# The running sum of exponentials on GpSimd, added in two halves instead of one

## The chip, the cores and the metric

The kernel runs on one core of a Trainium2 chip. The metric is the device time of one execution in microseconds (us); smaller is better. The engines are named as the profile names them: PE is TensorE (matmuls), PEld its weight loads, DVE is VectorE, ACT is ScalarE, POOL is GpSimd, SP is SyncE, which issues most of the DMAs.

## What is computed

One layer of an encoder is applied to two batches of 2048 tokens with the same weights: RMSNorm, one wide input projection, grouped-query attention (8 query heads, 2 key/value heads of 64) beside a Fourier branch, gates, an output projection, an embedding that is gated and added, and a final RMSNorm. The change lies in the softmax of the attention:

```python
def one_block(qblk):
    s = jnp.einsum('bkgqd,bskd->bkgqs', qblk, k).astype(jnp.float32) * scale
    pr = jax.nn.softmax(s, axis=-1).astype(v.dtype)
    return jnp.einsum('bkgqs,bskd->bqkgd', pr, v)
```

The kernel takes the softmax apart: it subtracts a maximum per query inside the matmul, makes the exponentials, multiplies them with the values without dividing, sums them beside that, and divides the product by the sum at the end.

## The kernel before

A first stage, up to about 760 us, loads and scales the weights, normalises the tokens and makes the projections. The second, from 760 to 2500 us, is the attention; the rest of the Fourier branch and the output projection are woven into it. A short tail finishes the last tokens.

The attention works through 64 **units**: a batch, a key/value head and a block of 128 tokens, that is 4 heads x 128 = 512 query columns. A unit has 8 **steps**, and each step takes 256 keys as two times 128. In `scores` a step makes two score tiles of 128x512 in PSUM by PE (line 1317, `ps_s`); ACT turns each into exponentials (line 1320), the first into `p[:, 0]`, the second into `p[:, 1]` of one float32 buffer of 128x2x512. There are seven such buffers (`P32`, tile `p32`), so step g takes the buffer of step g - 7.

POOL keeps the running sum. In step 0 it has nothing to do; in step 1 it adds the buffers of steps 0 and 1 into a fresh `acc` (line 1323), in steps 2 to 7 the new buffer to `acc` (line 1325), each time 128x1024 elements in one instruction. Behind step 7 three short instructions follow: line 1328 adds the two halves of `acc` to each other, 1329 and 1330 split the result into two float16 parts, `acc_h`. Four steps later, in step 4 of the next unit, PE sums `acc_h` over the partitions (`sums`, line 1399), and DVE takes the reciprocal and multiplies (`divide`, lines 1406 and 1407). The exponentials themselves go to PE in groups of four steps (`pv`, line 1383).

DVE takes the row maxima of a later unit (14 steps ahead) from PSUM (`maxima`, line 1355, tile `a_mx`): PE fills one buffer `ps_m` of two banks (line 1347), DVE reduces it, and only then can PE fill it again. Between these, DVE has work of the output projection. Three of its operations are 1024 columns wide and read two operands from SBUF: line 1554 (`mh`, the low part of the mixed branches), line 1703 (`h_hl`, the low part of the hidden state) and line 1689 (`h`, the final norm). `square` and `norm` with `rsqrt` (lines 269 to 284) make the factors of the norms in small operations of 128x2, on DVE for the first token block and at the very end, on POOL otherwise. POOL also multiplies a Fourier tile by its gate (line 1190, `fo`, 128x512, up to about 907 us) and the attention output by its gate (line 1535, `ag`, 128x512), and issues the stores of finished tokens (line 1691).

Each engine works through its instructions in the order in which they stand, and waits for semaphores of the others. In this stage the order on PE, ACT, DVE and SP is that in which the program writes it; that on POOL is made by the scheduler of the language.

Of the kernel before, what the change touches and what calls it, by code (L numbers as in the profile page):

```python
# [14 lines left out]
ALU = mybir.AluOpType  # L15
# [150 lines left out]
class Build:  # L166
# [1102 lines left out]
    def attention(self, kvp):  # L1269
# [3 lines left out]
        nc, st = self.nc, self.st  # L1273
# [3 lines left out]
        kt, vt, Q, P, O, MX, ACC, AT, M4, S, MR, AR = ({} for _ in range(12))  # L1277
# [28 lines left out]
        def scores(u, j):  # L1306
            s, kv, t = units[u]
            P[u, j] = p = pool.tile([128, 2, 512], F32, name="p32", bufs=P32)
            k = kt[s, kv, j // 4]
            todo = [] if j else [(kone, MR.pop(u))]  # L1310
            todo += [(k[:, j % 4, y], Q[u][b]) for y, b in ((1, 0), (1, 1), (2, 0))]
            if j == 0:
                S[u] = [self.psS.tile([128, 512], F32, name="ps_s") for e in range(2)]
            for i, (w, q) in enumerate(todo):
                for e in range(2):
                    sl = slice(64 * e, 64 * e + 64)
                    nc.tensor.matmul(S[u][e][:], w[sl], q[sl].rearrange("p h q -> p (h q)"), start=j == i == 0,  # L1317
                                     stop=i + 1 == len(todo), skip_group_check=True)
            for e in range(2):
                nc.scalar.activation(p[:, e, :], S[u][e][:], AF.Exp, scale=self.sc["s_scale"][:])  # L1320
            if j == 1:
                ACC[u] = pool.tile([128, 2, 512], F32, name="acc", bufs=2)
                nc.gpsimd.tensor_tensor(out=ACC[u][:], in0=P[u, 0][:], in1=p[:], op=ALU.add)  # L1323
            elif j > 1:
                nc.gpsimd.tensor_tensor(out=ACC[u][:], in0=ACC[u][:], in1=p[:], op=ALU.add)  # L1325
            if j == 7:
                acc, AR[u] = ACC.pop(u), pool.tile([128, 2, 512], F16, name="acc_h", bufs=1)
                nc.gpsimd.tensor_tensor(out=acc[:, 0, :], in0=acc[:, 0, :], in1=acc[:, 1, :], op=ALU.add)
                nc.gpsimd.tensor_copy(AR[u][:, 0, :], acc[:, 0, :])
                nc.gpsimd.tensor_tensor(out=AR[u][:, 1, :], in0=acc[:, 0, :], in1=AR[u][:, 0, :], op=ALU.subtract)  # L1330
                del Q[u], S[u]
                if u == last[s, kv]:
                    for b in range(2):
                        del kt[s, kv, b]
# [117 lines left out]
        for g in range(8 * n + 7):  # L1452
            self.step = g
            self.flush()
            u, j = g // 8, g % 8
            if j == 0 and 0 < u and u + 2 < n:
                load_q(u + 2)
            if g == 6:
                load_v(0, 1)
            if j == 4 and u - 1 in fresh:  # L1460
                load_kv(1, fresh[u - 1])
            if 0 <= u < n:
                scores(u, j)
            self.drain(lead(g))
            if j == 4:
                if u + 1 < n:
                    max_rows(u + 1)
                if u > 0:
                    ps = self.bank() if u < n else self.psM.tile([128, 1024], F32, name="ps_m")
                    sums(u - 1, ps[:, 0:256])  # L1470
                    divide(u - 1, ps[:, 0:256])
            heavy = (g - 1) % PVG == PVG - 1 and 0 <= g - 1 < 8 * n
            if heavy:
                self.run_slow(1 if j else 2)
                pv((g - 1) // 8, (g - 1) % 8 - PVG + 1)
            yield 0 if heavy else RATE if g >= 8 * n // 2 else 1 if g > FIRST else SLOW
# [567 lines left out]
```

## Time and profile before

| what | value |
|---|---|
| three runs | 2596.09, 2598.25, 2606.04 us (median 2598.25) |
| the profiled execution | 2597.87 us |
| its span, first to last instruction | 2595.8 us |
| mean granted clock of PE | 0.991 |
| POOL additions of line 1325 | 384, together 927.6 us |
| POOL additions of line 1323 | 64, together 150.8 us |
| exponentials of line 1320 on ACT | 1024, 684 ns each in the mean |
| maxima of line 1355 from `ps_m` on DVE | 498, 1223 ns each in the mean |

A row of a group or of the timeline names the line of the program, the engine, the operation, and what is written from what with its shape. A number in brackets at the end of a row of the timeline is the time for which the engine had been idle, with what ended it. Two instructions of POOL can overlap a little in the record, so what POOL takes for a series is read from the distance of the starts.

### The profile page before, as it was taken

Reading aid. Unit: us, or ns where it says so; the run is one execution under the profiler, and the core shown is the slowest. Engines: PE = TensorE matmul, PEld = TensorE weight load, DVE = VectorE, ACT = ScalarE, POOL = GpSimd, SP = SyncE. Lnnn points to the kernel's source line nnn. Section 1 sums busy time; section 2 is a strip of 40 time slices with the busy share of each in tenths; the row PEclk is TensorE's granted clock in tenths of the full one; section 3 lists DMA queues with packets and bytes.
Section 4 is the critical chain, followed back from the end, with each engine's and each line's share of the span. In section 5 each row is a group of like instructions: output and inputs, shape, how many; then the busy total and the mean of one; then the engine's idle time right before and its main releaser. Section 6 shows DMA issues by size and latency. Waiting matters only on the chain. (4 is left out here: it accounts for less than half of the span.)

```text
span 2595.8 us, 49879 instructions
## 1 busy us (share of the span) xinstructions
PE 2511.0 (97%) x19896; PEld 1384.0 (53%) x19896; DVE 1668.4 (64%) x2382; ACT 1183.6 (46%) x1983; POOL 1896.6 (73%) x1646
## 2 busy tenths in 40 slices
PE   6999989999999999999999999999999999999988
PEld 3566656666656545545545555445544554545533
DVE  7766576777566856566666666666666665766534
ACT  4433353434235545554544545444544444445522
POOL 0465545475659978888888888878887988888840
PEclk9999999999999999999999999999999999999999
DMA  8467588787377742223222233422223322233232
GB/s 259 101 175 198 162 223 230 185 195 180 103 197 248 212 118 62 58 76 78 59 69 75 71 81 88 90 69 63 73 73 82 72 75 63 66 82 76 78 76 53
DMA packets 450265, 297.92 MB, mean 115 GB/s; under 512 B 294000, under 2 KB 394480, under 8 KB 450032
## 3 DMA queue, kind: packets, MB, share of 16 engines
q1 hardware_dynamic: 437952, 256.28, 38.9%
q0 software_dynamic: 12080, 38.46, 4.2%
q8 instruction: 155, 2.54, 0.4%
q14 instruction: 78, 0.64, 0.1%
HBM read 146.12 MB, written 82.45 MB: 88 GB/s over the span
## 5 line engine op out<-in xcount | busy, mean ns | idle before, releaser
L1325 POOL TENSOR_TENSOR acc<-acc,p 128x1024 f32<-128x1024 f32 x384 | 927.6, 2416 | 109.5 <-ACT p L1320 84.6
L1320 ACT ACTIVATE p<-ps_s,s_scale 128x512 f32<-128x512 f32 x1024 | 648.1, 684 | 636.4 <-PE ps_s L1317 613.9
L1355 DVE TENSOR_REDUCE a_mx<-ps_m 128x1 f32<-128x1024 f32 x498 | 608.9, 1223 | 512.0 <-PE ps_m L1347 501.0
L1649 PE MATMUL ps_g<-w_pg,hT 64*128 64x512 f16 x2784 | 494.1, 376 | 3.8 <-DVE seen L1610 2.4
L1383 PE MATMUL ps_o<-p,v 128*64 128x256 f32 x4096 | 468.2, 381 | 0.0
L1317 PE MATMUL ps_s<-q,k 64*128 64x512 f16 x3072 | 433.1, 378 | 1.4 <-ACT p L1320 1.0
L1383 PEld LDWEIGHTS ps_o<-p,v 128*64 128x64 f32 x4096 | 283.7, 137 | 160.4 <-issue 28.5
L504 PEld LDWEIGHTS <-uc 128*128 128x128 f16 x2400 | 236.3, 99 | 231.2 <-DMA uc<-hl 19.5
L1649 PEld LDWEIGHTS <-hT 64*128 64x128 f16 x2784 | 204.8, 94 | 156.9 <-issue 15.7
L1649 PE MATMUL ps_g<-w_wo,mh 64*128 64x512 f16 x1440 | 260.5, 376 | 3.2 <-DVE mh L1554 1.9
L1649 PE MATMUL ps_g<-w_wo,mT 64*128 64x512 f16 x1440 | 257.3, 376 | 0.0
L1317 PEld LDWEIGHTS <-k 64*128 64x128 f16 x3072 | 152.6, 94 | 195.3 <-issue 77.0
L1347 PE MATMUL ps_m<-k,q 64*128 64x512 f16 x996 | 200.8, 377 | 10.2 <-DVE a_mx L1355 9.8
L504 PEld LDWEIGHTS <-w_ga 128*128 128x128 f16 x1536 | 148.8, 98 | 33.5 <-issue 11.9
L1323 POOL TENSOR_TENSOR acc<-p,p 128x1024 f32<-128x1024 f32 x64 | 150.8, 2357 | 11.7 <-ACT p L1320 10.7
L1649 PEld LDWEIGHTS <-mh 64*128 64x128 f16 x1440 | 101.5, 94 | 91.5 <-issue 16.6
L1649 PEld LDWEIGHTS <-mT 64*128 64x128 f16 x1440 | 107.0, 94 | 76.3 <-issue 4.8
L772 POOL TENSOR_TENSOR t<-t,t 128x640 f32<-128x640 f32 x32 | 49.2, 1556 | 121.2 <-DVE t L767 121.2
L1406 DVE RECIPROCAL ps_f<-ps_f 128x256 f32<-128x256 f32 x61 | 107.1, 1756 | 13.6 <-PE ps_f L1399 13.6
L504 PE MATMUL ps_x<-uc,w_ga 128*128 128x256 f16 x1008 | 113.5, 273 | 2.0 <-DVE a_mx L1355 1.4
L504 PE MATMUL ps_x<-w_gf,uc 128*128 128x512 f16 x480 | 108.0, 384 | 2.4 <-DVE a_mx L1355 2.4
L1390 ACT ACTIVATE at<-ps_o,a_scale 128x256 f32<-128x256 f32 x64 | 30.4, 474 | 168.2 <-PE ps_o L1383 168.2
(347 smaller groups left out, 3415.6 us busy)
## 6 DMA issues: line engine op xcount, KB each, us to landing
q<-qTd SPq DMA_DIRECT2D x256, 64.0 KB, 2.2
ag<-agd SPq DMA_DIRECT2D x64, 256.0 KB, 3.5
out<-h POOLq DMA_DIRECT2D x31, 512.0 KB, 3.1
x<-in_x_prompt SPq DMA_DIRECT2D x16, 512.0 KB, 4.9
gfd<-gt POOLq DMA_DIRECT2D x32, 256.0 KB, 2.7
agd<-gat POOLq DMA_DIRECT2D x64, 128.0 KB, 2.8
w_st<-in_w_out SPq DMA_DIRECT2D x32, 256.0 KB, 4.0
w_st<-in_w_ple_gate SPq DMA_DIRECT2D x32, 256.0 KB, 4.0
```

Source lines behind the costliest of these rows:

```text
L504: self.nc.tensor.matmul(ps, lhs(ia, k), rhs(ib, k), start=(i == 0), stop=(i == 3 * ks - 1))
L772: nc.gpsimd.tensor_tensor(out=t1[:, tt], in0=t1[:, tt], in1=t2[:, tt], op=ALU.add)
L1317: nc.tensor.matmul(S[u][e][:], w[sl], q[sl].rearrange("p h q -> p (h q)"), start=j == i == 0, stop=i + 1 == len(todo), skip_group_check=True)
L1320: nc.scalar.activation(p[:, e, :], S[u][e][:], AF.Exp, scale=self.sc["s_scale"][:])
L1323: nc.gpsimd.tensor_tensor(out=ACC[u][:], in0=P[u, 0][:], in1=p[:], op=ALU.add)
L1325: nc.gpsimd.tensor_tensor(out=ACC[u][:], in0=ACC[u][:], in1=p[:], op=ALU.add)
L1347: nc.tensor.matmul(ps[c], Q[u][0][sl, h, :], kt[s, kv, half][sl, :, 0, :], start=True, stop=True)
L1355: nc.vector.reduce_max(MX[u][:, h, half, c:c + 1], x, axis=AX.X)
L1383: nc.tensor.matmul(o[64 * f:64 * f + 64], vt[s, kv, c // 8][:, c % 8, :], p[:, e, f], start=(c == 0), stop=(c == 15))
L1390: nc.scalar.activation(at[:].rearrange("p c q -> p (c q)"), o, AF.Copy, scale=self.sc["a_scale"][:])
L1406: nc.vector.reciprocal(r, r)
L1649: nc.tensor.matmul(g[0][:], g[1](ia, k)[sl], g[2](ib, k)[sl], start=a, stop=z, skip_group_check=True)
```

## The change

Each addition of 128x1024 becomes two of 128x512: one adds `p[:, 0]`, one adds `p[:, 1]`, each to its half of `acc`. The arithmetic is the same. Lines behind it move by one (1328 becomes 1329, 1355 becomes 1356, and so on).

```diff
             if j == 1:
                 ACC[u] = pool.tile([128, 2, 512], F32, name="acc", bufs=2)
-                nc.gpsimd.tensor_tensor(out=ACC[u][:], in0=P[u, 0][:], in1=p[:], op=ALU.add)
-            elif j > 1:
-                nc.gpsimd.tensor_tensor(out=ACC[u][:], in0=ACC[u][:], in1=p[:], op=ALU.add)
+            if j:
+                a, b = ACC[u], P[u, 0] if j == 1 else ACC[u]
+                for e in range(2):
+                    nc.gpsimd.tensor_tensor(out=a[:, e], in0=b[:, e], in1=p[:, e], op=ALU.add)
             if j == 7:
                 acc, AR[u] = ACC.pop(u), pool.tile([128, 2, 512], F16, name="acc_h", bufs=1)
```

POOL before, the end of one unit and the beginning of the next, with the semaphores that an instruction waits for (Activation is ACT's, Pool its own; the number behind `p` is that of a buffer):

```order
L1325 TENSOR_TENSOR acc<-acc,p_10762 128x1024 [waits Activation_49,Pool_49]
L1535 TENSOR_TENSOR ag<-ag 128x512 [waits DMAHW2_49,DMAHW1_49,DVE_49]
L1325 TENSOR_TENSOR acc<-acc,p_10796 128x1024 [waits Activation_49,Pool_49]
L1325 TENSOR_TENSOR acc<-acc,p_10854 128x1024 [waits Activation_49,Pool_49]
L1328 TENSOR_TENSOR acc<-acc 128x512 [waits Pool_49]
L1329 CAST acc_h<-acc 128x512 [waits PE_49,Pool_49]
L1330 TENSOR_TENSOR acc_h<-acc,acc_h 128x512 [waits Pool_49]
L1323 TENSOR_TENSOR acc<-p_10903,p_10938 128x1024 [waits Activation_49]
```

The same place of POOL with the change:

```order
L1326 TENSOR_TENSOR acc<-acc,p_10808 128x512 [waits Activation_49,Pool_49] x2
L1536 TENSOR_TENSOR ag<-ag 128x512 [waits DMAHW2_49,DMAHW1_49,DVE_49]
L1326 TENSOR_TENSOR acc<-acc,p_10843 128x512 [waits Activation_49,Pool_49] x2
L1326 TENSOR_TENSOR acc<-acc,p_10902 128x512 [waits Activation_49,Pool_49] x2
L1329 TENSOR_TENSOR acc<-acc 128x512 [waits Pool_49]
L1330 CAST acc_h<-acc 128x512 [waits PE_49,Pool_49]
L1331 TENSOR_TENSOR acc_h<-acc,acc_h 128x512 [waits Pool_49]
L1326 TENSOR_TENSOR acc<-p_10952,p_10987 128x512 [waits Activation_49] x2
```

Each addition has become two that stand next to each other, and nothing else has moved. A half waits on ACT for its own exponential, and on POOL for its own half of the step before, which is the second instruction back.

At three places of the first units a product of the Fourier branch came to stand between two halves. POOL before, at one of them:

```order
L1325 TENSOR_TENSOR acc<-acc,p_10252 128x1024 [waits Activation_49,Pool_49]
L1190 TENSOR_TENSOR fo<-fo,gf_in 128x512 [waits DMAHW6_49,DVE_49]
L1325 TENSOR_TENSOR acc<-acc,p_10274 128x1024 [waits Activation_49,Pool_49]
L1190 TENSOR_TENSOR fo<-fo,gf_in 128x512 [waits DMAHW7_49,DMAHW3_49,DVE_49]
L1328 TENSOR_TENSOR acc<-acc 128x512 [waits Pool_49]
```

POOL there with the change:

```order
L1326 TENSOR_TENSOR acc<-acc,p_10285 128x512 [waits Activation_49,Pool_49] x2
L1326 TENSOR_TENSOR acc<-acc,p_10308 128x512 [waits Activation_49,Pool_49]
L1190 TENSOR_TENSOR fo<-fo,gf_in 128x512 [waits DMAHW6_49,DVE_49]
L1190 TENSOR_TENSOR fo<-fo,gf_in 128x512 [waits DMAHW7_49,DMAHW3_49,DVE_49]
L1326 TENSOR_TENSOR acc<-acc,p_10308 128x512 [waits Activation_49,Pool_49]
L1329 TENSOR_TENSOR acc<-acc 128x512 [waits Pool_49]
```

The first product has moved behind one half, the second ahead of one. Beside three products of line 1190 one of line 1535 has moved by one half. On PE, ACT, DVE and SP every instruction stands where it stood, with the same waits; only line and buffer numbers differ.

## The prediction

> **What bounds the kernel now.** I read the page's first part, then the busy time by stretches, then who waited for whom on PE.
>
> ```profile
> span 2595.8 us, 49879 instructions
> PE 2511.0 (97%) x19896; PEld 1384.0 (53%) x19896; DVE 1668.4 (64%) x2382; ACT 1183.6 (46%) x1983; POOL 1896.6 (73%) x1646
> ...
> 1000.00:1500.00 500.00, 495.10 (x4350) 255.32 (x4348) 322.07 (x303) 249.84 (x413) 435.59 (x349) 1.00 0.27 68
> 1500.00:2000.00 500.00, 496.60 (x4358) 246.73 (x4356) 314.10 (x286) 247.87 (x406) 421.86 (x368) 1.00 0.32 78
> 2000.00:2500.00 500.00, 498.37 (x4376) 252.23 (x4372) 308.51 (x272) 243.69 (x400) 427.48 (x358) 1.00 0.29 71
> ```
>
> The columns of the last three rows are busy time of PE, PEld, DVE, ACT and POOL, then the granted clock and DMA. The attention stage runs from 760 to 2500 us and holds every instruction that changes. PE is busy 1490.1 of these 1500 us, POOL 1284.9 (86%): POOL is second, and neither DVE (63%) nor ACT (49%) is near. So the change can bring only what PE still waits, and cost only what makes PE wait anew.
>
> ```profile
> PE ps_m L1347 <- DVE a_mx L1355: 6.3, 10, 1.6
> PE ps_s L1317 <- ACT p L1320: 5.0, 4, 4.0
> PE ps_g L1649 <- DVE mh L1554: 1.9, 3, 0.8
> PE ps_g L1649 <- DVE h L1570: 0.5, 2, 0.3
> ...
> PE ps_m L1347 <- DVE a_mx L1355: 3.4, 7, 0.9
> ```
>
> These are PE's waits (us in total, times, longest), first from 930 to 2500 us, and as the last row the largest of 760 to 930. After 930 PE waits 13.7 us in all, and no row names POOL.
>
> **Part one: what the halves cost on POOL.** 448 additions of 1024 columns become 896 of 512.
>
> ```profile
> L1325 POOL TENSOR_TENSOR acc<-acc,p x384: 2340/2353/3439, 771.7 to 2492.0; 128x1024 f32<-128x1024 f32 x192
> L1323 POOL TENSOR_TENSOR acc<-p,p x64: 2336/2357/2379, 766.1 to 2475.0; 128x1024 f32<-128x1024 f32 x64
> L1190 POOL TENSOR_TENSOR fo<-fo,gf_in x32: 1262/1272/1282, 774.0 to 907.1; 128x512 f32<-128x512 f32 x32
> ...
> 774.01 2.50 POOL L1190 TENSOR_TENSOR fo<-fo,gf_in 128x512 f32<-128x512 f32 x2
> 776.47 2.37 POOL L1325 TENSOR_TENSOR acc<-acc,p 128x1024 f32<-128x1024 f32 x1
> ...
> 781.24 7.22 POOL L1325 TENSOR_TENSOR acc<-acc,p 128x1024 f32<-128x1024 f32 x3
> ...
> 793.33 1.26 POOL L1328 TENSOR_TENSOR acc<-acc 128x512 f32<-128x512 f32 x1
> 794.66 0.61 POOL L1329 CAST acc_h<-acc 128x512 f16<-128x512 f32 x1
> ```
>
> By durations the halves look dear: 2 x 1.272 = 2.54 us against 2.353. What counts on a full queue is the spacing. Three additions in a row take 7.22 us, 3 x 2.353 plus two gaps of 0.08: each reads what the one directly ahead wrote. L1328 and L1329, also dependent, leave a gap of 0.07. The two products of L1190 are independent and take 2.50 together, so the second starts 0.04 ahead of the first one's end; from the first of the pair to the next instruction it is 776.47 - 774.01 = 2.46 us. In the changed order a half depends on its own half of the step before, two instructions back. I therefore price a pair at 2.46 against 2.353 + 0.08 = 2.43: +0.03 us a step, 448 x 0.03 = 13 us of POOL time, 0.2 us a unit of seven additions. If every half had the dependent gap, a pair would be 2 x (1.272 + 0.07) = 2.68: +0.25 a step, 1.8 us a unit. Below nothing: with an empty queue the first half starts behind the first of two exponentials, and the last half ends earlier than a whole addition would. I take +0.03, by the nearest row, of the same shape, type and spacing.
>
> The Trainium skill, GPSIMD Engine Reference, section 3.1 "Elementwise — side-by-side cycle accounting", speaks against halving: each instruction pays a dispatch through two software hops, and an element of a two-input operation about 2.6 cycles at 1.2 GHz. By that, 512 columns are 1.11 us, an estimate; the trace's 1.272 leaves 0.16 for the fixed part, and 448 more of them would be some 72 us of POOL time, 1.1 us a unit. The spacing of the L1190 pair says that most of it is hidden behind the instruction ahead.
>
> A unit takes (2475.0 - 766.1) / 63 = 27.1 us, and POOL is idle in 14% of it, 3.9 us. Either price fits. Nor does lateness reach PE:
>
> ```profile
> 2012.94 1.16 POOL L1330 TENSOR_TENSOR acc_h<-acc,acc_h 128x512 f16<-128x512 f32 x1
> ...
> 2014.69 2.38 POOL L1323 TENSOR_TENSOR acc<-p,p 128x1024 f32<-128x1024 f32 x1
> ...
> 2014.71 0.41 PE L1399 MATMUL ps_f<-acc_h,ones 128*64 128x256 f16 x4
> ...
> 2025.18 1.27 ACT L1320 ACTIVATE p<-ps_s,s_scale 128x512 f32<-128x512 f32 x2 [1.04 <-PE ps_s L1317]
> ```
>
> POOL's result goes to PE's sums (L1399), four steps into the next unit, and frees the buffers of the exponentials. This is the tightest place of the 64 units: L1330 ends at 2014.10, PE reads at 2014.71, 0.6 us later. Seven steps on from the buffer that L1323 read, ACT writes it again, 8.1 us after L1323 left it at 2017.07. +0.2 us fits; at +1.8 the tightest units would cost PE about a us each, 5 us for a handful.
>
> **Part two: what the halves free on DVE.**
>
> ```profile
> L1703 DVE SCALAR_TENSOR_TENSOR h_hl<-h,h_r,h_hl 128x1024 f16<-128x1024 f32 x29 | 65.3, 2251 | 1.3 <-ACT h_hl L1699 1.3
> L1554 DVE SCALAR_TENSOR_TENSOR mh<-ag,mix_s,mh 128x1024 f16<-128x1024 f32 x30 | 62.4, 2079 | 0.0
> L1689 DVE SCALAR_TENSOR_TENSOR h<-h,rsh_z,gfin 128x1024 f32<-128x1024 f32 x27 | 61.6, 2280 | 0.0
> ...
> 958.49 1.28 DVE L1703 SCALAR_TENSOR_TENSOR h_hl<-h,h_r,h_hl 128x1024 f16<-128x1024 f32 x1 [1.28 <-ACT h_hl L1699]
> ...
> 1221.20 4.80 POOL L1325 TENSOR_TENSOR acc<-acc,p 128x1024 f32<-128x1024 f32 x2
> 1223.85 3.23 DVE L1703 SCALAR_TENSOR_TENSOR h_hl<-h,h_r,h_hl 128x1024 f16<-128x1024 f32 x1
> 1226.08 2.13 POOL L1328 TENSOR_TENSOR acc<-acc 128x512 f32<-128x512 f32 x1
> 1227.01 2.28 DVE L1689 SCALAR_TENSOR_TENSOR h<-h,rsh_z,gfin 128x1024 f32<-128x1024 f32 x1
> 1229.22 1.21 DVE L1355 TENSOR_REDUCE a_mx<-ps_m 128x1 f32<-128x1024 f32 x1
> 1230.48 0.39 PE L1347 MATMUL ps_m<-k,q 64*128 64x512 f16 x2 [1.56 <-DVE a_mx L1355]
> ...
> 1518.97 0.39 PE L1347 MATMUL ps_m<-k,q 64*128 64x512 f16 x2 [1.56 <-DVE a_mx L1355]
> ```
>
> With POOL idle, L1703 takes 1.28 us; its mean after 930 is 2.25. At 1223.85 it starts just behind the start of POOL's second addition (about 1223.65), sits until that ends at 1226.0 and then runs; L1328 is held in turn, 2.13 instead of 1.27. L1355 stands behind both DVE operations, and PE behind L1355: 1.56 us, and once more as long at 1518.97. With halves, the operation waits for a half of 1.27 at most: one that arrives in the first half is through 1.2 us sooner, one that arrives in the second as now.
>
> This is the rule of the Trainium skill, SBUF — State Buffer, "Who interferes with whom": a VectorE instruction with two SBUF inputs contends with a GpSimd one that reads SBUF, and whoever is first keeps the shared port for its whole instruction. The trace agrees (3.23 against 1.28).
>
> Two halves without a gap between them could shut DVE out for both. A boundary without a gap is in the trace:
>
> ```profile
> 2002.85 2.27 POOL L1535 TENSOR_TENSOR ag<-ag 128x512 f32<-128x512 f32 x1 [4.95 <-DVE a_mx L1355]
> 2003.90 2.30 DVE L1689 SCALAR_TENSOR_TENSOR h<-h,rsh_z,gfin 128x1024 f32<-128x1024 f32 x1
> 2005.08 3.33 POOL L1325 TENSOR_TENSOR acc<-acc,p 128x1024 f32<-128x1024 f32 x1
> ```
>
> L1325 starts 0.04 ahead of L1535's end, yet L1689 ends at 2006.20 and L1325 takes 3.33: DVE had its turn first.
>
> The sum, from the waits after 930. L1347 on L1355, 6.3 us in 10: the two long ones of 1.56 lose 1.2 each, the other eight have 3.2 us between them, 0.4 each, and go. L1649 on L1554 and L1570, 2.4 us in 5, all under 1.2, go. Of L1317's 4.0 us 1.2 goes, since there a small operation of the norm chain on DVE, 0.16 us when nothing holds it, sat through one addition:
>
> ```profile
> 953.89 2.34 POOL L1325 TENSOR_TENSOR acc<-acc,p 128x1024 f32<-128x1024 f32 x1
> 953.98 2.27 DVE L279 SCALAR_TENSOR_TENSOR rsh_z<-rsh_t,rsh_z 128x2 f32<-128x2 f32 x1
> ...
> 956.67 0.16 DVE L279 SCALAR_TENSOR_TENSOR rsh_w<-rsh_t,rsh_z 128x2 f32<-128x2 f32 x1
> ```
>
> Together 2.4 + 3.2 + 2.4 + 1.2 = 9.2 us if each came in the first half. Some don't, and L1328, as short before as after, holds others; I take three quarters, 7 us. For the 3.4 us before 930 I count nothing. PE, ACT, DVE and SP keep their order; on POOL four products move past one half addition, 1.2 us either way, and none of them is waited for by PE in these rows. The profiled execution took 2597.87 us, its span and 2.1 around it: 2597.9 - 7 = **2591 us**. The median of the three runs is 2598.25, 0.4 above it, so the same number stands against both.
>
> **The rivals.** First, DVE is freed, but PE gets nothing: each unit lines DVE and POOL up anew, and new waits replace the old. For it: DVE is idle a third of the time and most blocked operations make nobody wait (86 of those three lines, 15 waits). Against it: no wait behind one addition can be as long as before. Time: 2598. Second, more is freed than PE's rows show: all 13.7 us of waiting after 930 go and the 3.4 before: 2581. Third, slower: a half costs what L1328 does on average, not at its median.
>
> ```profile
> L1328 POOL TENSOR_TENSOR acc<-acc 128x512 f32<-128x512 f32 x64 | 95.9, 1499 | 4.9
> ```
>
> Then a pair is 3.00 us, +0.57 a step, 4.0 us a unit, just past POOL's free 3.9; with the gap of 0.07 for each half it is +0.71, 5.0 a unit, 1.1 too much in each of 64, +70 us. The place is the sums at L1399, the point from which it decides 3.9 / 7 = 0.56 us a step; between the two I put it at 2630. Against it: L1328's mean is so high because DVE operations fall on it (2.13 above against 1.27), and they are no more than before. That the change doesn't do what it says is excluded: in the changed order each half stands by itself, with a wait of its own on ACT.
>
> **How the numbers follow.** Forecast (5 to 10 us gained) 0.55, at 2591; nothing gained 0.30, at 2598; all gained 0.09, at 2581; POOL late 0.06, at 2630. The range takes in the forecast, the first rival and, with the runs' own spread of a few us, half of the second: 2584 to 2602. About 0.5% is what a measurement of this kernel can tell from no change, 13 us: faster than 2585 needs the second rival, 0.08; slower than 2611 the third, 0.05; within, 0.87.
>
> **What would show it.** Halves spaced 1.23 us in a full queue (wrong from 1.5 on); the means of L1703, L1554 and L1689 falling from 2.1-2.3 to about 1.7 us; PE's waits on L1355 after 930 falling from 6.3 us to 2-3, none on POOL; POOL's busy time up by 10 to 80 us. A new row of PE behind POOL at L1399, or DVE means that don't fall, would make the prediction wrong.

## The result, and the profile after

| | median | runs | ratio to before (95% interval) |
|---|---|---|---|
| before | 2597.44 us | 4, 2596.09 to 2606.04 | |
| with the halves | 2632.65 us | 4, 2623.02 to 2636.48 | 1.0125 (1.011 to 1.0141) |

The change makes the kernel 1.25% slower; 2591 us was predicted, in a range of 2584 to 2602. The profiled execution of after is the fastest of its four runs, 2623.02 us.

First the page of after:

```profile
span 2621.2 us, 50690 instructions
PE 2517.3 (96%) x19896; PEld 1384.7 (53%) x19896; DVE 1665.7 (64%) x2382; ACT 1182.6 (45%) x1983; POOL 1952.5 (74%) x2094
```

Then its busy time by stretches, with the same columns as before (PE, PEld, DVE, ACT and POOL, then granted clock and DMA):

```profile
1000.00:1500.00 500.00, 499.34 (x4386) 258.12 (x4380) 314.48 (x307) 253.08 (x418) 458.58 (x497) 1.00 0.27 69
1500.00:2000.00 500.00, 488.39 (x4280) 241.96 (x4278) 310.72 (x281) 241.11 (x396) 428.29 (x477) 0.99 0.31 78
2000.00:2500.00 500.00, 475.23 (x4101) 237.43 (x4098) 307.34 (x260) 229.87 (x379) 412.93 (x464) 0.97 0.26 67
```

Read it against the three rows of before, stretch by stretch: from 1000 to 1500 PE is busy 4.2 us more than before, a gain of the kind that was forecast; from 1500 on it is busy 8.2 and then 23.1 us less. DVE is no fuller than before in those late stretches, and POOL's change (6.4 us more, then 14.6 less) is small: PE isn't held by an engine that has run full.

PE's waits (us in total, times, longest) over the window that the prediction used, 930 to 2500 us:

```profile
PE ps_m L1348 <- DVE a_mx L1356: 36.3, 10, 7.4
PE ps_s L1317 <- ACT p L1320: 2.0, 5, 0.8
```

Its first row again, from 930 to 1500 us:

```profile
PE ps_m L1348 <- DVE a_mx L1356: 1.4, 2, 1.2
```

And from 1500 to 2500 us:

```profile
PE ps_m L1348 <- DVE a_mx L1356: 34.8, 8, 7.4
```

Of 13.7 us in all before, it is now 39.0: 25.3 more, and the profiled execution is 25.2 us longer. The loss stands in PE's waits behind one thing, the maxima on DVE, and there in eight waits after 1500 us. POOL is named in no row.

The POOL additions, with shortest, median and longest duration in ns:

```profile
L1326 POOL TENSOR_TENSOR acc<-acc,p x768: 1249/1267/2320, 767.1 to 2519.6; 128x512 f32<-128x512 f32 x192
L1326 POOL TENSOR_TENSOR acc<-p,p x128: 1255/1271/1288, 763.7 to 2503.1; 128x512 f32<-128x512 f32 x128
```

And the three wide DVE operations from 930 to 2500 us, with busy time and mean:

```profile
L1555 DVE SCALAR_TENSOR_TENSOR mh<-ag,mix_s,mh 128x1024 f16<-128x1024 f32 x28 | 88.3, 3152 | 0.0
L1690 DVE SCALAR_TENSOR_TENSOR h<-h,rsh_z,gfin 128x1024 f32<-128x1024 f32 x26 | 51.4, 1975 | 0.0
L1704 DVE SCALAR_TENSOR_TENSOR h_hl<-h,h_r,h_hl 128x1024 f16<-128x1024 f32 x28 | 45.8, 1635 | 1.3 <-ACT h_hl L1700 1.3
```

`h` and `h_hl` fell (2280 to 1975, 2251 to 1635), where about 1.7 us was forecast for all three. `mh` rose from 2079 to 3152. A mean hides how: the shortest, median and longest `mh` are 1277, 1628 and 10471 ns, so most are faster than before and a few are very long. This is the longest, in the timeline (start, duration, both in us):

```profile
2008.10 2.51 POOL L1326 TENSOR_TENSOR acc<-p,p 128x512 f32<-128x512 f32 x2
2010.56 12.27 POOL L1326 TENSOR_TENSOR acc<-acc,p 128x512 f32<-128x512 f32 x10
...
2013.44 10.47 DVE L1555 SCALAR_TENSOR_TENSOR mh<-ag,mix_s,mh 128x1024 f16<-128x1024 f32 x1
2023.84 1.21 DVE L1356 TENSOR_REDUCE a_mx<-ps_m 128x1 f32<-128x1024 f32 x1
...
2025.10 0.61 PE L1348 MATMUL ps_m<-k,q 64*128 64x512 f16 x2 [6.96 <-DVE a_mx L1356]
```

Ten halves run on POOL from 2010.56 to 2022.83, spaced (12.27 - 1.25) / 9 = 1.22 us, none with a gap. `mh` starts in the middle, and ends at 2023.91, 1.08 us behind the last of them: that is its own work, done once POOL had stopped. It passed seven boundaries between halves without getting in. L1356 stands behind it on DVE, and PE behind L1356 for 6.96 us. Eight `mh` took longer than one half and their own 1.28 us: 10.24 us at 1590.64, 6.19 at 1817.46, 10.47 at 2013.44, 3.38 at 2076.91, 2.60 at 2133.41, 10.21 at 2187.21, 9.37 at 2251.40 and 6.76 at 2314.67. Six of them stand ahead of PE's waits of 2.7 to 7.4 us, together 33.7.

A long wait has a second price. PE's clock ahead of this one, just behind it, and then:

```profile
2003.00:2017.00 14.00, 14.00 (x124) 6.71 (x122) 10.86 (x10) 6.77 (x11) 13.75 (x14) 1.00 0.24 57
2025.10:2028.20 3.10, 3.05 (x16) 1.18 (x17) 1.83 (x2) 0.00 (x0) 0.00 (x0) 0.54 0.52 127
2028.20:2033.00 4.80, 4.80 (x46) 2.30 (x44) 1.35 (x2) 1.56 (x3) 3.05 (x3) 1.00 0.18 55
```

For 3.1 us PE has 0.54 of its clock, which costs 3.1 x 0.46 = 1.4 us. The clock was low like this behind five of the six waits, from the one of 3.3 us up; behind the shortest, 2.7 us, it stayed at 1.00. PE's busy time rose by 6.3 us for the same 19896 matmuls (2511.0 to 2517.3), which with 19.1 us more of idle time makes up the 25.4 by which the span grew; the waits of the window alone make 25.3, so outside of it PE idled 6.2 us less.

### The profile page after: what moved, and what is told of

Same layout as the page of the kernel before. It is cut to its first block, busy times and chain, and to the rows that moved or that the text cites. A ratio compares the mean times of both kernels' runs of the same rounds, so it can differ in the third digit from the quotient of the medians.

```text
span 2621.2 us, 50690 instructions
## 1 busy us (share of the span) xinstructions
PE 2517.3 (96%) x19896; PEld 1384.7 (53%) x19896; DVE 1665.7 (64%) x2382; ACT 1182.6 (45%) x1983; POOL 1952.5 (74%) x2094
## 5 line engine op out<-in xcount | busy, mean ns | idle before, releaser
L1326 POOL TENSOR_TENSOR acc<-acc,p 128x512 f32<-128x512 f32 x768 | 988.6, 1319 | 89.1 <-ACT p L1320 88.7
L1356 DVE TENSOR_REDUCE a_mx<-ps_m 128x1 f32<-128x1024 f32 x498 | 608.7, 1222 | 536.5 <-PE ps_m L1348 526.2
L1650 PE MATMUL ps_g<-w_pg,hT 64*128 64x512 f16 x2784 | 501.8, 381 | 3.9 <-DVE seen L1611 2.4
L1348 PE MATMUL ps_m<-k,q 64*128 64x512 f16 x996 | 201.2, 379 | 38.3 <-DVE a_mx L1356 38.2
L1326 POOL TENSOR_TENSOR acc<-p,p 128x512 f32<-128x512 f32 x128 | 159.8, 1271 | 11.2 <-ACT p L1320 10.6
L1348 PEld LDWEIGHTS <-q 64*128 64x128 f16 x1024 | 60.7, 94 | 101.2 <-issue 49.7
```

Of the source, the lines that this page charges most:

```text
L1326: nc.gpsimd.tensor_tensor(out=a[:, e], in0=b[:, e], in1=p[:, e], op=ALU.add)
L1348: nc.tensor.matmul(ps[c], Q[u][0][sl, h, :], kt[s, kv, half][sl, :, 0, :], start=True, stop=True)
L1356: nc.vector.reduce_max(MX[u][:, h, half, c:c + 1], x, axis=AX.X)
L1650: nc.tensor.matmul(g[0][:], g[1](ia, k)[sl], g[2](ib, k)[sl], start=a, stop=z, skip_group_check=True)
```

## The experiments

The question was what shuts `mh` out. **Theory A**: POOL's halves follow each other without a gap, since none reads what the one directly ahead wrote, and DVE's operation with two operands in SBUF doesn't get in between them. **Theory B**: twice as many instructions of half the size cost by themselves. Ratios are to the kernel before, timed on the same chip.

### A gap in every step: in even steps the second exponential and the second half come first

```diff
-            for e in range(2):
+            for e in ((1, 0) if j and j % 2 == 0 else (0, 1)):
...
-                for e in range(2):
+                for e in ((0, 1) if j % 2 else (1, 0)):
```

> The halves stay, but in every even step the second tile is made and added first, so that the first half of a step depends on the instruction directly ahead on POOL; the gap of 0.08 us comes back once a step. Theory A (DVE is shut out by a series of POOL instructions without gaps): the longest of the mh operation on DVE falls from 10.5 us to under 4, PE's waits on a_mx from 38 to about 10 us, the time is that of before, 2590 to 2602. Theory B (896 short instructions cost POOL and its neighbours more than 448 long ones): as with the change, 2623 to 2640.

Measured: 2589.76 us, ratio 0.9954 (0.9938 to 0.997). PE's waits on the maxima from 760 to 2520 us, in which the changed kernel has 38.2:

```profile
PE ps_m L1348 <- DVE a_mx L1356: 4.8, 8, 1.5
```

The instructions of `mh` (shortest, median and longest in ns):

```profile
L1555 DVE SCALAR_TENSOR_TENSOR mh<-ag,mix_s,mh x32: 1277/1513/2290, 894.0 to 2511.4; 128x1024 f16<-128x1024 f32 x32
```

As many halves, of the same size, on a POOL that is busier than after (1976.1 us against 1952.5), and no `mh` over 2.3 us. B falls. The time is just below the range that was expected, which was that of the kernel before: this kernel is 0.46% faster than before as well.

### No gaps with whole additions: two running sums, taken in turns

```diff
+            if j in (1, 3):
+                ACC[u, j] = pool.tile([128, 2, 512], F32, name=f"acc{j}", bufs=1)
+                nc.gpsimd.tensor_tensor(out=ACC[u, j][:], in0=P[u, j - 1][:], in1=p[:], op=ALU.add)
+            elif j > 3:
+                a = ACC[u, 3 if j % 2 else 1]
+                nc.gpsimd.tensor_tensor(out=a[:], in0=a[:], in1=p[:], op=ALU.add)
+            if j == 7:
+                a, b = ACC.pop((u, 1)), ACC.pop((u, 3))
+                nc.gpsimd.tensor_tensor(out=a[:], in0=a[:], in1=b[:], op=ALU.add)
```

> The additions are 128x1024 again and as many as before, but go to two running sums in turn, so that each depends on the second instruction back and the gaps go. Theory A: the mh operation is shut out as with the change or longer (over 8 us at the longest), PE's waits on a_mx are 25 to 60 us, the time is 2615 to 2650. Theory B: count and size of before, 2592 to 2602.

Measured: 2629.24 us, ratio 1.0108 (1.0083 to 1.0134). The same two rows of this kernel, first of PE's waits:

```profile
PE ps_m L1352 <- DVE a_mx L1360: 35.6, 27, 6.8
```

Then of `mh`:

```profile
L1559 DVE SCALAR_TENSOR_TENSOR mh<-ag,mix_s,mh x32: 1277/2345/10380, 896.7 to 2554.8; 128x1024 f16<-128x1024 f32 x32
```

No instruction was halved, their count and size are those of before, and it is as slow as the change, with an `mh` of 10.4 us. So halving isn't needed for the loss. It is spread otherwise than in the change: two waits of 6.8 and 6.4 us stand behind the two `mh` of about 10 us, and the other 22 us are 25 waits of up to 3.0 us. The edit also moves additions within a unit (none in step 2, one more at the end), and no run separates that from the missing gap.

### `mh` off DVE, with halves and with whole additions

```diff
-                nc.vector.scalar_tensor_tensor(out=mh[:, 1], in0=ag, scalar=msc[:], in1=mh[:, 0],
-                                               op0=ALU.mult, op1=ALU.subtract)
+                nc.scalar.activation(mh[:, 1], ag, AF.Copy, scale=msc[:])
```

> The changed kernel, but the low part mh is written by ACT as a second copy of the scaled branch instead of by DVE as a difference (the low part of the output projection's input is therefore left out). The mh operation on DVE is gone, its 1.15 us are on ACT. Theory A, with mh as the only operation that is shut out for long: PE's waits on a_mx are under 10 us and the time is 2585 to 2600. Theory B, or if other DVE operations are shut out as well: 2615 to 2640.

> The control of the run before it: the kernel before, whole additions, with the same edit at mh (its low part is left out of DVE, ACT writes the scaled product there instead). If the series of halves costs only because mh is shut out by it, then with mh off DVE whole additions and halves should stand close together: 2575 to 2588 us, at most 0.4% above the halves' 2576.8, since here the long waits behind one whole addition of 2.35 us (L1689, L1703) remain. PE's waits on the maxima 3 to 8 us. If more and shorter instructions on POOL cost time by themselves, whole additions with mh off DVE are 1% faster than halves with it: 2545 to 2560 us.

Measured: with halves 2576.75 us, ratio 0.9906 (0.9877 to 0.9935); with whole additions 2580.84, ratio 0.9918 (0.9899 to 0.9937). The row of PE for the maxima from 760 to 2520 us, first with halves, then with whole additions:

```profile
PE ps_m L1348 <- DVE a_mx L1356: 3.5, 8, 1.1
```

```profile
PE ps_m L1347 <- DVE a_mx L1355: 6.9, 10, 2.2
```

The 1.25% between the two kernels is gone once this one operation leaves DVE: the intervals overlap. The whole loss goes through `mh`. The kernel with halves came out below the range that was expected for it, and both are faster than before by 0.8 to 0.9%: with `mh` gone DVE has less to do, whatever POOL does.

### A gap behind every half: 512 and 513 columns that share one, the sum in two buffers in turns

```diff
-                for e in range(2):
-                    nc.gpsimd.tensor_tensor(out=a[:, e], in0=b[:, e], in1=p[:, e], op=ALU.add)
+                b, a = P[u, 0] if j == 1 else ACC[u], pool.tile([128, 2, 512], F32, name="acc", bufs=2)
...
+                for sl in (slice(0, 512), slice(511, 1024)):
+                    nc.gpsimd.tensor_tensor(out=a[:, sl], in0=b[:, sl], in1=c[:, sl], op=ALU.add)
```

> The halves overlap by one column (512 and 513 columns into a fresh buffer each step), so that every half depends on the one directly ahead and a gap of 0.08 us stands behind each. Theory A: no DVE operation waits longer than for one half, the three wide operations have means of 1.6 to 1.9 us and 2.7 at most, PE's waits on a_mx fall below those of before (9.8 us) to 3 to 7, the time is 2588 to 2597; POOL is 80 to 120 us busier in its distances and still has room. Theory B: more POOL time than with the change, 2630 or more.

Measured: 2595.75 us, ratio 0.9977 (0.9962 to 0.9992), `mh` at most 2.3 us, and PE's waits on the maxima 4.4 us from 760 to 2520 us, as expected; only the mean of `h`, 1.98 us, is above its range. PE's waits from 930 to 2500 us:

```profile
PE ps_s L1317 <- ACT p L1320: 6.0, 4, 4.9
PE ps_f L1400 <- POOL acc_h L1331: 2.7, 3, 0.9
...
PE ps_m L1348 <- DVE a_mx L1356: 0.3, 1, 0.3
```

From 930 us on the maxima hold almost nobody. The second row is the one of which the prediction warned, PE behind POOL at the sums: with a gap behind each half POOL is late in three units, by up to 0.9 us.

### A gap in every second step

From here on the halves stay in their order, and a gap is made where the first half is one column longer, since it then reads a column that the half directly ahead wrote.

```diff
-                for e in range(2):
-                    nc.gpsimd.tensor_tensor(out=a[:, e], in0=b[:, e], in1=p[:, e], op=ALU.add)
+                a, b, c = [x[:].rearrange("p e q -> p (e q)") for x in (a, b, p)]
+                m = 512 if j % 2 else 513
+                for sl in (slice(0, m), slice(m, 1024)):
+                    nc.gpsimd.tensor_tensor(out=a[:, sl], in0=b[:, sl], in1=c[:, sl], op=ALU.add)
```

> A dose between the changed kernel and the one with a gap in every step: in even steps the first half is one column longer (0:513 and 513:1024), so it reads the column that the half directly ahead wrote and waits for it; POOL's gapless series is at most four halves, some 4.9 us. If what counts is how long a gapless series runs, the longest mh is 5.5 to 6.5 us and not 10.5, PE's waits on the maxima are 6 to 20 us between 760 and 2520 (38 in the changed kernel, 4.8 with a gap in every step), and the time lies between those two kernels: 2592 to 2615 us. If the length of the series doesn't matter and the number of halves does, it is as slow as the changed kernel, 2620 to 2636 us.

Measured: 2585.27 us, ratio 0.9937 (0.9919 to 0.9955). PE's waits on the maxima, from 760 to 2520 us:

```profile
PE ps_m L1350 <- DVE a_mx L1358: 4.7, 9, 1.4
```

The instructions of `mh`:

```profile
L1557 DVE SCALAR_TENSOR_TENSOR mh<-ag,mix_s,mh x32: 1278/1683/2365, 890.0 to 2506.5; 128x1024 f16<-128x1024 f32 x32
```

Theory A as I had it missed here: I expected `mh` to be held over up to four halves, and none was; the longest, 2.37 us, is its own 1.28 and less than one half. Waits and time are below the ranges expected. So it isn't only that DVE slips through the gap itself: in these short series it also got in at the boundaries without one.

### Other tiles at `mh`'s place

```diff
-                nc.vector.scalar_tensor_tensor(out=mh[:, 1], in0=ag, scalar=msc[:], in1=mh[:, 0],
-                                               op0=ALU.mult, op1=ALU.subtract)
+                nc.scalar.activation(mh[:, 1], ag, AF.Copy, scale=msc[:])
+                if t:
+                    other = pool.tile([128, DM], F16, name="other", bufs=1)
+                    nc.vector.scalar_tensor_tensor(out=other[:], in0=gfin[:], scalar=msc[:],
+                                                   in1=wp[0][:, 0].rearrange("p k q -> p (k q)"),
+                                                   op0=ALU.mult, op1=ALU.subtract)
```

> The changed kernel; mh's low part is left out (ACT writes the scaled product there), and at its place on DVE stands an operation of the same form and size on other tiles (other = gfin times a factor minus a weight tile, 128x1024 float16 out). It asks whether mh's own operands or its place make it lose to POOL's series. If the place and moment decide, the substitute is shut out as mh was, for 5 to 10.5 us some five to nine times, PE waits 20 to 40 us on the maxima and the time is 2610 to 2640 us. If the operands decide (the tile ag, which POOL has just written, or mh itself), no substitute is longer than 3.9 us, PE's waits on the maxima stay at 3 to 8 us and the time is 2575 to 2595 us.

Measured: 2624.24 us, ratio 1.0095 (1.0082 to 1.0109). PE's waits on the maxima, from 760 to 2520 us:

```profile
PE ps_m L1348 <- DVE a_mx L1356: 30.4, 14, 7.8
```

The instructions of the substitute:

```profile
L1558 DVE SCALAR_TENSOR_TENSOR other<-gfin,mix_s,wp x31: 1277/1645/10618, 930.5 to 2516.2; 128x1024 f16<-128x1024 f32 x31
```

The substitute, which reads neither `ag` nor `mh` (only the factor `mix_s` is the same), is shut out as `mh` was, for up to 10.6 us. It isn't the operands `ag` and `mh`; it is the place in the program at which the operation meets POOL.

### What a boundary looks like where DVE loses

Two neighbouring halves overlap by some ns in the records: the next one starts before the last one is recorded as ended. In unit 46 of the changed kernel, that of the timeline above, the overlaps of a half with the one ahead are 51, 49, 39, 32, 32, 31 ns and then stay at 31 to 33. It is so in many units: behind a gap the overlap starts at 40 to 60 and falls to 31 to 33 within some five to seven halves, if no DVE operation comes in between. It isn't so in all: at the seventh boundary of the series of the changed kernel in which no half had been held up, 20 of 33 overlaps are 33 ns or less. I call a series that has come to that **settled**.

From the timelines of seven kernels with halves (the change, the gap in every step, `mh` off DVE, the gap in every second step, other tiles, and the two below) I took each case from 760 us on in which one of the wide DVE operations had started at least 0.11 us ahead of a boundary without a gap between two halves, and looked at the first such boundary. "Got in" means that the operation ended within 1.7 us of it:

| | overlap 34 ns or more | 33 ns or less |
|---|---|---|
| `mh`, or the substitute in its place | got in 64 of 66 times | 0 of 22 |
| `h` and `h_hl` | 179 of 179 | 13 of 13 |

At `mh`'s place the overlap splits the cases almost cleanly; once shut out there, it also stayed out at the next settled boundaries (59 of 62). `h` and `h_hl` got in either way. So a settled series goes with being shut out, but isn't all of it.

It is a correlation, and weaker than the table looks. The 24 cases at `mh`'s place that were shut out are the same eight places of the program in three kernels. One of the two exceptions is the `mh` of 10.24 us at 1590.64 in the changed kernel: it met 41 ns and stands ahead of PE's longest wait. The overlap is that of the very boundary that was won or lost; by the boundary ahead of it, up to which the operation had waited 0.11 us at most, 17 of 18 were shut out behind 33 ns or less and 7 of 34 behind more. And the count of halves since the gap splits the same cases: at `mh`'s place all 57 got in at the first three boundaries and 24 of 29 were shut out at the fourth to seventh, where `h` and `h_hl` got in 55 of 55 times. The last two kernels test the place of a single gap; they can't tell the overlap from that count.

### One gap in a unit, in step 3 or in step 5

Against the kernel with a gap in every second step:

```diff
-                m = 512 if j % 2 else 513
+                m = 513 if j == 3 else 512
```

The second kernel has `j == 5` there.

> The changed kernel with one gap in a unit: in step 3 the first half is one column longer (0:513 and 513:1024), so it waits for the half directly ahead, and behind it ten halves run without a gap. In the changed kernel and in the one with other tiles the rows show that the overlap of neighbouring halves falls from 55 ns behind a gap to 31 to 33 ns some five halves later, that mh is shut out where it meets 31 to 33 ns, and that it comes four to six halves into a unit. First reading (a series must settle before it shuts DVE out): behind this gap mh meets an unsettled series, at most two shut-outs of over 4 us, PE waits 3 to 15 us on the maxima between 760 and 2520 us, time 2585 to 2602 us. Second reading (only the halves that still stand ahead count): mh, which comes just behind the gap, is held until the series ends, up to nine halves, 10 us, PE waits 25 to 40 us, time 2615 to 2636 us.

> The same with the gap in step 5: eight halves run ahead of it, and mh comes in the fifth to seventh of them. Both readings let it be shut out there, but only until the gap: the longest mh 4 to 5.5 us, PE's waits on the maxima 5 to 15 us between 760 and 2520 us (each wait at most 2 us), time 2588 to 2606 us. If the gap doesn't let DVE in, and mh waits for the end of the unit's additions, it is as slow as the changed kernel, 2620 to 2636 us, with mh up to 10 us.

Measured: gap in step 3 2585.07 us, ratio 0.9936 (0.9915 to 0.9957); gap in step 5 2599.78 us, ratio 0.9999 (0.9985 to 1.0013). The timeline at the same place as above (unit 46), with the gap in step 3:

```profile
2001.59 14.62 POOL L1328 TENSOR_TENSOR acc<-acc,p 128x512 f32<-128x512 f32 x11
...
2004.25 2.25 DVE L1557 SCALAR_TENSOR_TENSOR mh<-ag,mix_s,mh 128x1024 f16<-128x1024 f32 x1
```

PE's waits on the maxima in that kernel, from 760 to 2520 us:

```profile
PE ps_m L1350 <- DVE a_mx L1358: 4.7, 8, 1.3
```

The timeline of the same place with the gap in step 5:

```profile
2012.80 12.04 POOL L1328 TENSOR_TENSOR acc<-acc,p 128x512 f32<-128x512 f32 x9
...
2015.36 5.92 DVE L1557 SCALAR_TENSOR_TENSOR mh<-ag,mix_s,mh 128x1024 f16<-128x1024 f32 x1
```

All `mh` of that kernel:

```profile
L1557 DVE SCALAR_TENSOR_TENSOR mh<-ag,mix_s,mh x32: 1276/1625/6125, 894.2 to 2525.5; 128x1024 f16<-128x1024 f32 x32
```

And its row of PE for the maxima, from 760 to 2520 us:

```profile
PE ps_m L1350 <- DVE a_mx L1358: 15.1, 15, 3.3
```

With the gap in step 3, `mh` comes just behind it, with nine more halves standing ahead, and gets in at the first boundary, 2.25 us instead of 10.47. With the gap in step 5, it comes into the settled series ahead of the gap and is held until the gap, 5.92 us, no longer. The two longest, 5.92 and 6.13, and PE's longest wait of 3.3 are above what I had written (5.5 and 2); the one of 6.13 came in the fourth half, earlier in its unit than the rest. The time is in its range, and the sum of the waits, 15.1, at the end of its own. The second reading of the first of the two, by which only the halves ahead count, falls.

## Why the prediction was wrong

**The step that failed** is the cost of a hold, "With halves, the operation waits for a half of 1.27 at most", and with it the case of two halves without a gap between them, which "could shut DVE out for both". In the runs an operation of 1.28 us was held for up to 9.2 us, over seven boundaries. I had dismissed that case by one boundary, that of L1535 and L1325 at 2005 us, at which DVE had its turn first. That boundary was the first one behind a wait of POOL of 4.95 us, so it was of the kind at which DVE nearly always gets in, and it said nothing of the fifth or sixth half of a series. The kernel before has no such series: its additions all leave a gap. From it I went on to "no wait behind one addition can be as long as before", which held for `h`, `h_hl` and most `mh`; seven `mh` took longer (3.38 to 10.47 us) than the longest of before (3.26).

**The gap was priced from one side.** I counted the 0.08 us between two dependent additions as POOL time that the halves would save, and nothing else. It was also what gave DVE its turn, there and at the boundaries just behind it: with it in every step, in every second or in step 3 alone, 0.5 to 0.6% are gained; without it, in halves (1.0125) or whole (1.0108), 1.1 to 1.25% are lost. It has to stand where the operation comes: in step 5 it gained nothing (0.9999), and behind every half, where POOL came late at the sums, 0.23%.

**What held.** POOL's price: halves spaced 1.22 us where 1.23 was forecast, busy time up by 55.9 us, within 10 to 80. The margin of the sums: no PE wait behind POOL, so the rival that ended slower, at 2630 us, came close to the measured 2632.65 by luck; its place was the sums, and the loss came at the maxima. What shorter holds are worth: from 930 to 1500 us, where no `mh` was shut out, PE's wait of 4.0 us behind ACT is gone and the maxima cost 1.4 us instead of 2.8; and the halves with a gap in every step, in every second or in step 3 come out at 2585 to 2590 us on chips where before takes 2600 to 2601, so 11 to 16 us are gained where 7 were forecast.

**What was mis-sized** is the sum's largest term: PE's wait on the maxima, forecast to fall from 6.3 to 2-3 us, rose to 36.3.

The Trainium skill, SBUF — State Buffer, "Who interferes with whom", says of the shared port that whoever issues first has it for the whole instruction. I read that as: and gives it up behind it. That holds for the 243 cases of the table at 34 ns or more in which DVE got in; but in the timeline above GpSimd kept DVE out over seven boundaries between its instructions (10.47 us against 1.28 alone), and the measurement decides. The Trainium skill, GPSIMD Engine Reference, section 2.1 "Instruction dispatch", says that each of GpSimd's cores starts the next instruction as soon as its own share of the last is done, which agrees with the overlaps of 31 to 60 ns. No run here shows the cores one by one, so whether the overlap shrinks because they fall into step is not shown.

**What stays open**: what it is in a later part of a series that holds DVE out, the overlap, the count of halves or something that goes with both, and why `h` and `h_hl` got in at all 13 boundaries of 33 ns or less that they met, where an operation at `mh`'s place never did (0 of 22). No run shows how the port is granted.

## What to carry to other kernels

Before a long instruction is cut into pieces so that another engine may get in between, ask what lets it in: here it was the gap that a dependence leaves, with the boundaries just behind it, and the cut removed the dependence together with the length. When a rival is dismissed by one row, ask how that row's surroundings differ from those that the change makes. And look at an operation's longest duration beside its mean: six of 28 stood ahead of 33.7 of PE's 36.3 us.

## What was not expected of the hardware

- A DVE operation with two SBUF operands, 1.28 us alone, took up to 10.6 us beside GpSimd additions that follow each other without a gap. Such a hold ended at the next gap of 0.08 us (5.92 us with the gap in step 5).
- The first boundaries behind such a gap let it in as well: a gap in step 3 alone, or in every second step, did as much as one in every step (0.9936, 0.9937 and 0.9954).
- After PE had waited 6.96 us, its granted clock was 0.54 for 3.1 us, 1.4 us more on top of the wait; after a wait of 2.7 us it was 1.00.
- These three kernels, with a gap in every step, in every second or in step 3, are faster than both the kernel before and the change. The one with a gap in every second step, 2585.27 us, differs from the change only by the column at which the two halves of every second step are parted.
